# One hybrid decoder step: the scan of each SSD group cut anew

## The chip, the cores and the metric

The kernel runs on one core of a Trainium2 chip. TensorE (PE) multiplies matrices, VectorE (DVE) and ScalarE (ACT) work element by element, GpSimd (POOL) is a second, programmable element engine, and SyncE (SP) issues the DMA transfers. The metric is the device time of one execution in microseconds (us). Before the change, three runs have a median of 1921.59 us (1919.1 to 1923.15).

## What is computed

The reference is one layer of a decoder trunk on 256 prompt tokens (with 16 learned meta tokens ahead of them) and 8 x 8 sample tokens, all in float32. Cut to what matters:

```python
h = rms_norm(x, norm_w)
z, xbc, dt_raw, sc_b, sc_c, sc_h, sc_z, g_a, g_b = split_proj(h @ w_in)
xbc = silu(causal_dwconv(xbc, conv_prev, ssd_conv_w) + ssd_conv_b)
xs, bm, cm = split(xbc)                  # 64 heads x 64; 8 groups x 128 states
dt = softplus(dt_raw + dt_bias)
# per segment, chunk by chunk; acum is the running sum of dt * -exp(a_log):
y_diag = (cc . bc) * exp(seg) * dt  applied to xc        # inside the chunk
h_next = exp(acum[-1]) * h + sum(to_end * xc * bc)       # carried state
y_off  = exp(acum) * (cc . h)                            # from the state before
y = y_diag + y_off + d_skip * xs
y_a = group_rms_norm(y * silu(z)) @ w_ssd_out            # norm over 512 of one group
y_b = (sc_b * causal_dwconv(sc_c * sc_h) * silu(sc_z)) @ w_sconv_out
out = x + (sigmoid(g_a) * y_a + sigmoid(g_b) * y_b) @ w_o   # then a last rms_norm
```

The outputs also hold the new states: of the prompt, and of each of the 8 sample sequences (128 x 512 numbers a group and sequence).

## The kernel before

Activations lie transposed: 128 channels on the partitions, tokens along the columns. There are T = 336 columns: 16 meta, 256 prompt, 64 sample; TV = 320 leaves the meta tokens out. Each weight block of 128 x 1024 float32 is loaded by SyncE (`wraw`, L79), rounded by ScalarE to a high part (`whi`, L81), and VectorE makes the rest (`wlo`, L83); each has three buffers. A product is then three matmuls in fp32r, a single-pass form of float32: high by high (L89), high weight by low activation (L90), low weight by high activation (L93). One unit is 48 such matmuls.

The stage with the scan ("pb") has 8 groups of 8 heads. A group's units run in a fixed order: 4 z units (L407), 8 output units of the group before (L588; of two outputs of 24 matmuls each), and 6 conv units of the next group (L391: B, C, and four tiles of x). Group 0 has no output units; group 7 has 8 gate units (L602) in place of the conv units. The scan `ssd(g)` is a generator which yields between its steps, and `weave` (L619) runs some of its steps after each unit, `NSTEP` = 24 spread over the group's units. [...]

The scan cuts the 336 columns into three chunks of 128, 128 and 80: the first has meta and prompt, the third 16 prompt columns and the 64 sample columns. Its steps in order: `to_rows` (transposes x and B of a chunk into rows, L444, L448; `xdt` is x times dt), `weights` (the decay matrix `W`, loaded from DRAM and made by subtraction, exponent and the product with `cbm`, L462 to L465; `xe` on GpSimd, L467; `E` for the off-diagonal part of chunk 1), `inside` (the weighted sums, L477), `skip` (adds d_skip * x, L485), `carry` (the state, matmul L495, into `hst`). For the sample states `h0` (loaded at L432) the old state's contribution is taken by matmuls on `CZ` (L525; L528 does the same for the prompt columns of chunk 2), then GpSimd shrinks all eight states in place (L533), and the weighted sums of chunk 2 receive that contribution through the constant `C_SY` (L538).

The new sample states need, for each sequence, its 8 rows of x and B in four variants (high and low parts) at 32 partitions. Constant selection matrices (`sel`, matmuls L560, L561, L565, L566) do this on TensorE, for four sequences at a time. Then eight matmuls of 32 rows (L573), each with its addition to `h0` (L574), and the stores (L576), two sequences in each of four steps.

The group norm takes `zs[0]`, the sum of squares of 128 channels' lanes over four tiles. `rstd` (L105) sums over partitions by one-column matmuls (L111), so that 320 tokens lie as 112 x 3, scales them (L115, VectorE), raises them to -0.5 (L116, GpSimd), spreads them as diagonals (L121, VectorE) and multiplies by ones (L122) to have the factor in all partitions. Then y is scaled (L582) and split in high and low parts (`yh`, `yl`, L583, L584) for the output units.

PSUM has eight banks in four names of two: `pj` (projections), `ms` and `sg` (scan), `yb` (weighted sums).

Of the kernel before, what the change touches and what calls it, by code (L numbers as in the profile page):

```python
# [7 lines left out]
F32 = mybir.dt.float32  # L8
# [16 lines left out]
NSTEP = 24  # L25

C_ID, C_U, C_M1, C_UQ, C_M1Q, C_ONE = 0, 128, 256, 384, 464, 544
C_SX, C_SE, C_SY, C_SEG = 672, 1696, 1824, 1904
C_ALL = 1912
# [13 lines left out]
def tile_hybrid_step(ctx, tc, xT, w1, w2, wdt, wso, wsc, wo, cmask, vec, hvec, convst, sconvst, h0T,  # L43
# [11 lines left out]
    sg_d = dr.tile([KT, P, TV], F32, name="sg_d")  # L55

# [68 lines left out]

    def run(gen):
# [15 lines left out]
    with tc.tile_pool(name="pa", bufs=2) as pa:  # L142
# [31 lines left out]
        def eights(ap, w=8):  # L174
            return ap.rearrange("p (b t) -> p b t", t=w)

# [44 lines left out]
        consts(0, C_SX)  # L221
# [26 lines left out]
        for j in range(KT):  # L248
            u = (up0, ups0) if j == 0 else u1 if j == 1 else conv_in(j, proj)
            if j == 3:  # L250
                nc.sync.dma_start(HV, hvec)
                consts(C_SX, C_SE)
# [98 lines left out]
    def sel(kind, u):  # L351
        o = C_SX + (2 * kind + u) * P
        return CR[:80, o:o + P]

# [3 lines left out]
    with tc.tile_pool(name="pb", bufs=2) as pb:  # L358
# [4 lines left out]
        CZ = pb.tile([P, 288], F32, name="CZ", bufs=1)  # L363
        nc.gpsimd.memset(CZ, 0.0)
        czs = CZ[:, 0:256].rearrange("p (q w) -> p q w", w=64)
# [57 lines left out]
        def ssd(g, st):  # L423
# [4 lines left out]
            nc.gpsimd.tensor_copy(CZ[:, 272:288], CT[:, 256:272])  # L428
            h0, h0t = [], []
            for u in range(4):  # L430
# [4 lines left out]
            ys = [pb.tile([P, TV], F32, name="ys", bufs=4) for _ in range(4)]  # L435
            W, xdt, xe, bt, cbm, yb = [None] * 3, [None] * 3, [None] * 3, None, None, [None] * 3

            def to_rows(c):
                t0, n = CH[c]
                W[c] = pb.tile([P, 8, P], F32, name="W")  # L440
                nc.sync.dma_start(W[c][:n, :, :n], ac_d[c][8 * g:8 * g + 8, :].partition_broadcast(n))
                pp = ps.tile([P, 512], F32, name="ms")
                for t in range(4):
                    nc.tensor.transpose(pp[:n, t * P:t * P + P], xs[:, t, t0:t0 + n], ident)  # L444
                xdt[c] = big("xdt", 2)
                nc.vector.tensor_tensor(split(xdt[c][:n]), split(pp[:n]), bc(hv(dtt[:n, c, :], g), [n, 8, HP]), mult)
                pq = ps.tile([P, 512], F32, name="ms")
                nc.tensor.transpose(pq[:n, 0:P], BT[:, t0:t0 + n], ident)  # L448
                nc.tensor.matmul(pq[:n, P:P + n], BT[:, t0:t0 + n], CT[:, t0:t0 + n], start=True, stop=True)
                bt = pb.tile([P, P], F32, name="bt", bufs=1)  # L450
                nc.scalar.activation(bt[:n], pq[:n, 0:P], AF.Copy)
                cbm = pb.tile([P, P], F32, name="cbm")
                nc.vector.tensor_tensor(cbm[:n, :n], pq[:n, P:P + n], U if c < 2 else UQ, mult)
                return bt, cbm

            def weights(c):
                n, w = CH[c][1], W[c]
                if c == 1:
                    nc.scalar.activation(E, w, AF.Exp)
                    nc.gpsimd.tensor_tensor(E, E, bc(CT[:, P:2 * P].unsqueeze(1), [P, 8, P]), mult)  # L460
                for h in range(8):
                    nc.vector.tensor_scalar(w[:n, h, :n], w[:n, h, :n], act[:n, c, 8 * g + h:8 * g + h + 1], 0.0,  # L462
                                            sub, ALU.min)
                nc.scalar.activation(w[:n, :, :n], w[:n, :, :n], AF.Exp)
                nc.vector.tensor_tensor(w[:n, :, :n], w[:n, :, :n], bc(cbm[:n, :n].unsqueeze(1), [n, 8, n]), mult)  # L465
                xe[c] = big("xe", 2)
                nc.gpsimd.tensor_tensor(split(xe[c][:n]), split(xdt[c][:n]), bc(hv(tet[:n, c, :], g), [n, 8, HP]), mult)  # L467

            def inside(c):
                n = CH[c][1]  # L470
                yb[c] = ps.tile([P, 512], F32, name="yb")
                for t in range(4):
                    lhs = [(xdt[c][:n], W[c][:n, :, :n])] + ([(hst, E)] if c == 1 else [])
                    for i, (x, w) in enumerate(lhs):
                        for q in range(2):
                            h = 2 * t + q
                            nc.tensor.matmul(yb[c][q * HP:(q + 1) * HP, t * n:t * n + n],  # L477
                                             x[:, h * HP:(h + 1) * HP], w[:, h, :],
                                             start=t == 0 and i == 0, stop=t == 3 and i == len(lhs) - 1 and c < 2)

            def skip(c):
                t0, n = CH[c]
                i0 = META if c == 0 else 0
                for t in range(4):
                    nc.vector.scalar_tensor_tensor(ys[t][:, t0 + i0 - META:t0 + n - META],  # L485
                                                   xs[:, t, t0 + i0:t0 + n], col(V_D, 4 * g + t),
                                                   yb[c][:, t * n + i0:t * n + n], mult, add)

            def carry(c):
                hn = big("hst", 2)  # L490
                if c:
                    nc.gpsimd.tensor_tensor(split(hn), split(hst), bc(hv(cdec[:, c - 1, :], g), [P, 8, HP]), mult)
                r = CH[c][1] if c < 2 else META
                pst = ps.tile([P, 512], F32, name="sg")
                nc.tensor.matmul(pst, bt[:r], xe[c][:r], start=True, stop=True)  # L495
                if c == 0:
                    nc.scalar.activation(hn, pst, AF.Copy)
                else:
                    nc.vector.tensor_tensor(hn, hn, pst, add)
                return hn  # L500

            E = pb.tile([P, 8, P], F32, name="E", bufs=1)
            bt, cbm = to_rows(0)
# [3 lines left out]
            hst = carry(0)  # L507
            bt, cbm = to_rows(1)
            yield
            weights(1)  # L510
            yield
            yield
            inside(0)
            inside(1)
            skip(0)
            skip(1)
            yield
            hst = carry(1)
            bt, cbm = to_rows(2)
            yield  # L520
            weights(2)
            pp = ps.tile([P, 512], F32, name="ms")
            for s_ in range(2):
                for q in range(4):
                    nc.tensor.matmul(pp[32 * q:32 * q + 32], CZ[:, 64 * q + 32 * s_:64 * q + 32 * s_ + 32],  # L525
                                     h0[2 * q + s_], start=s_ == 0, stop=False)
            for q in range(4):
                nc.tensor.matmul(pp[32 * q:32 * q + 32, q * P:q * P + P], CZ[:, 256:288], hst[:, q * P:q * P + P],  # L528
                                 start=False, stop=True)
            yo = big("yo", 1)  # L530
            nc.vector.tensor_tensor(split(yo), split(pp), bc(hv(eaY, g), [P, 8, HP]), mult)
            for b in range(NB):
                nc.gpsimd.tensor_tensor(split(h0[b]), split(h0[b]), bc(hv(decS[:, b, :], g), [P, 8, HP]), mult)  # L533
            yield
            yield
            inside(2)
            for t in range(4):
                nc.tensor.matmul(yb[2][:, t * 80:t * 80 + 80], yo[:, t * P:t * P + P], CM[:, C_SY:C_SY + 80],  # L538
                                 start=False, stop=t == 3)
            yield  # L540
            nc.sync.dma_start(ssmp[g], carry(2))
            skip(2)
            xe = xe[2]
            xe2 = pb.tile([P, 2, 512], F32R, name="xe2", tag="W")
            xeh, xel = xe2[:, 0, :], xe2[:, 1, :]
            nc.scalar.activation(xeh[:80], xe[:80], AF.Copy)
            nc.vector.tensor_tensor(xel[:80], xe[:80], fb(xeh[:80]), sub)
            bhh = pb.tile([P, 2, P], F32R, name="bhh", bufs=1)
            nc.scalar.activation(bhh[:80, 0, :], bt[:80], AF.Copy)
            nc.vector.tensor_tensor(bhh[:80, 1, :], bt[:80], fb(bhh[:80, 0, :]), sub)  # L550
            zs = st["zs"]
            for t in range(4):
                nc.vector.tensor_tensor(ys[t], ys[t], zs[t], mult)  # L553
                nc.scalar.activation(zs[t], ys[t], AF.Square)
                if t:
                    nc.gpsimd.tensor_tensor(zs[0], zs[0], zs[t], add)
# [237 lines left out]
```

## Time and profile before

| | |
|---|---|
| median of three runs | 1921.59 us |
| profiled execution | 1921.81 us, its span 1920.0 us |
| mean granted TensorE clock | 0.994 |
| group 0, from its first matmul to that of group 1 | 96.4 us |
| groups 1 to 6, each | 119.1 to 119.2 us |
| group 7 | 118.7 us |

The span is the time from the first to the last instruction of one execution that the profiler recorded; the rest of its time lies around it. Rows of a timeline give start, duration, engine, line, operation, output <- inputs, shapes, and in brackets the idle time of the engine just before and what ended it. Matmuls overlap, so their durations are longer than the distance from one start to the next; the distance is what they cost. A group of instructions is given with its count and its shortest, median and longest duration in ns.

### The profile page before, as it was taken

To read this page: it belongs to the slowest core of one execution; us is meant where nothing else is said; L and a number is where in the kernel's file an instruction comes from. 1 tells how busy PE (TensorE), PEld (TensorE's weight loads), DVE (VectorE), ACT (ScalarE), POOL (GpSimd) and SP (SyncE) were. 2 spreads that over 40 slices of the span, in tenths; PEclk is the share of its full clock that TensorE was granted. 3 is DMA by queue.
4 is the path that set the end of the run, shared out by engine and by line. 5 is a ranking of instruction groups with operands and counts; after the bars stand their busy time and mean duration, and the time that the engine had idled before them with its cause. 6 is when DMAs were issued, how large, how long until landed. Compare 5 with 4: busy or idle time off the path is not lost.

```text
span 1920.0 us, 31901 instructions
## 1 busy us (share of the span) xinstructions
PE 1878.4 (98%) x12838; PEld 1818.0 (95%) x12838; DVE 1168.2 (61%) x1831; ACT 761.9 (40%) x1074; POOL 324.2 (17%) x397
## 2 busy tenths in 40 slices
PE   7999999999999999999999999999999998999996
PEld 7999999999999999898998989989899897999996
DVE  6745444444543337776667877677776777464543
ACT  6433333333333335354543534335353442333432
POOL 0100000000000002323213232133321332000011
PEclk9999999999999999999999999999999999999998
DMA  6444444444444455363645546455364652665553
GB/s 215 152 158 153 145 152 147 150 145 155 149 157 151 161 179 190 123 222 128 232 140 192 180 127 224 148 190 175 131 227 141 199 171 93 194 225 167 169 176 106
DMA packets 102948, 318.69 MB, mean 166 GB/s; under 512 B 16144, under 2 KB 29072, under 8 KB 102800
## 3 DMA queue, kind: packets, MB, share of 16 engines
q1 hardware_dynamic: 102800, 316.65, 50.2%
q8 instruction: 101, 1.65, 0.3%
q14 instruction: 47, 0.39, 0.1%
HBM read 290.28 MB, written 26.32 MB: 165 GB/s over the span
## 4 chain that ended last, share of the span: by engine, by line
PE 61%; DVE 5%; issue 1%; ACT 1%; DMA 1%; POOL 0%; SPq 0%; DVEq 0%; ACTq 0%
PE pj L89 19%; PE pj L90 18%; PE pj L93 18%; DVE wlo L83 1%; PE yb L477 1%; PE sg L495 1%; DVE ys L553 1%; PE ms L525 1%; DVE W L462 1%; PE sg L573 1%; DMA W<-ac_d 1%; ACT whi L81 0%; PE ms L444 0%; PE ms L122 0%; DVE ya L599 0%
## 5 line engine op out<-in xcount | busy, mean ns | idle before, releaser
L83 DVE TENSOR_TENSOR wlo<-wraw,whi 128x1024 fp32r<-128x1024 f32 x481 | 603.4, 1255 | 509.1 <-PE pj L93 315.3
L89 PE MATMUL pj<-hhi,whi 128*128 128x320 f32 (+3 forms) x2960 | 892.9, 313 | 0.0
L90 PE MATMUL pj<-hlo,whi 128*128 128x320 f32 (+3 forms) x2960 | 887.7, 312 | 0.0
L81 ACT ACTIVATE whi<-wraw 128x1024 fp32r<-128x1024 f32 x481 | 508.8, 1058 | 881.1 <-PE pj L90 809.5
L89 PEld LDWEIGHTS pj<-hhi,whi 128*128 128x128 f32 x2960 | 556.1, 188 | 4.4 <-issue 3.9
L90 PEld LDWEIGHTS pj<-hlo,whi 128*128 128x128 f32 x2960 | 555.2, 188 | 1.0 <-issue 0.7
L93 PE MATMUL pj<-hhi,wlo 128*128 128x320 f32 (+3 forms) x2960 | 501.1, 311 | 0.0
L93 PEld LDWEIGHTS pj<-hhi,wlo 128*128 128x128 f32 x2960 | 455.5, 188 | 0.5 <-issue 0.2
L89 PE MATMUL pj<-yh,whi 128*128 128x320 f32 x512 | 159.2, 322 | 10.6 <-DVE ya L599 9.5
L90 PE MATMUL pj<-yl,whi 128*128 128x320 f32 x512 | 153.1, 310 | 0.0
L89 PEld LDWEIGHTS pj<-yh,whi 128*128 128x128 f32 x512 | 96.7, 189 | 24.2 <-issue 18.3
L90 PEld LDWEIGHTS pj<-yl,whi 128*128 128x128 f32 x512 | 96.9, 189 | 0.0
L93 PE MATMUL pj<-yh,wlo 128*128 128x320 f32 x512 | 96.4, 310 | 0.0
L381 DVE SCALAR_TENSOR_TENSOR cacc<-pad,V,cacc 128x360 f32<-128x360 f32 (+1 forms) x144 | 86.4, 600 | 14.9 <-ACT cacc L379 11.5
L533 POOL TENSOR_TENSOR h<-h,decS 128x512 f32<-128x512 f32 x64 | 81.6, 1308 | 9.9 <-PE ms L525 9.9
L192 POOL COPY SCS<-up 128x2 f32<-128x2 f32 x16 | 20.5, 1281 | 368.8 <-DVE up L186 365.8
L93 PEld LDWEIGHTS pj<-yh,wlo 128*128 128x128 f32 x512 | 80.8, 189 | 0.2 <-issue 0.2
L599 DVE TENSOR_TENSOR ya<-ya,pj 128x320 f32<-128x320 f32 x112 | 54.0, 482 | 37.0 <-PE pj L93 36.8
L90 PE MATMUL pj<-vlo,whi 128*128 128x320 f32 x256 | 75.5, 309 | 0.0
L89 PE MATMUL pj<-vhi,whi 128*128 128x320 f32 x256 | 75.5, 309 | 0.0
L375 POOL COPY cs<-pad 128x3 f32<-128x3 f32 x48 | 30.6, 638 | 249.0 <-ACT pad L372 249.0
L462 DVE TENSOR_SCALAR W<-W,act 128x128 f32<-128x128 f32 (+1 forms) x192 | 55.0, 341 | 8.8 <-DMA W<-ac_d 8.0
(205 smaller groups left out, 1571.6 us busy)
## 6 DMA issues: line engine op xcount, KB each, us to landing
wraw<-w SPq DMA_DIRECT2D x352, 512.0 KB, 3.9
wraw<-wso SPq DMA_DIRECT2D x64, 512.0 KB, 3.5
wraw<-wsc SPq DMA_DIRECT2D x32, 512.0 KB, 3.7
h<-h0T SPq DMA_DIRECT2D x32, 512.0 KB, 5.4
ssms<-h SPq DMA_DIRECT2D x32, 512.0 KB, 4.7
wraw<-wo SPq DMA_DIRECT2D x32, 512.0 KB, 3.8
W<-ac_d SPq DMA_DIRECT2D x16, 512.0 KB, 6.2
mb_d<-thg SPq DMA_DIRECT2D x16, 160.0 KB, 1.8
```

The source lines that it names most:

```text
L81: nc.scalar.activation(hi[:, :n], raw[:, :n], AF.Copy)
L83: nc.vector.tensor_tensor(lo[:, :n], raw[:, :n], fb(hi[:, :n]), sub)
L89: nc.tensor.matmul(out, w, xh(k0 + k), start=first and k == 0, stop=False)
L90: nc.tensor.matmul(out, w, xl(k0 + k), start=False, stop=False)
L93: nc.tensor.matmul(out, w, xh(k0 + k), start=False, stop=last and k == nk - 1)
L192: nc.gpsimd.tensor_copy(SCS[:, j, 0, :], up[:, 256:258])
L375: nc.gpsimd.tensor_copy(cs[:, 0, :], pad[:, 272:275])
L381: nc.vector.scalar_tensor_tensor(acc[:, i0:], pad[:, i0 + k:360 + k], col(V_CW, 4 * j + k), acc[:, i0:], mult, add)
L462: nc.vector.tensor_scalar(w[:n, h, :n], w[:n, h, :n], act[:n, c, 8 * g + h:8 * g + h + 1], 0.0, sub, ALU.min)
L477: nc.tensor.matmul(yb[c][q * HP:(q + 1) * HP, t * n:t * n + n], x[:, h * HP:(h + 1) * HP], w[:, h, :], start=t == 0 and i == 0, stop=t == ...
L533: nc.gpsimd.tensor_tensor(split(h0[b]), split(h0[b]), bc(hv(decS[:, b, :], g), [P, 8, HP]), mult)
L599: nc.vector.tensor_tensor(ya[:, m, :TV], ya[:, m, :TV], pp[:, :TV], add)
```

## The change

The scan is cut into other steps, with `NSTEP` = 22:

- **One visit for all weighted sums.** The sums of the three chunks run together (L538 of the changed kernel, and L542 for the sample part) after both states are there; the banks of `yb` are one tile of two banks, and chunk 2 uses a bank of `sg`. Its part from the state before, formerly by `CZ`, now uses `E2`, an exponential matrix of 16 columns made like `E`. The d_skip additions follow (L545, L553).
- **Rows replicated through DRAM.** The high and low parts of x and B are written twice to `xq_d` and `bq_d` (L561, L562) and read back as tiles with the four variants (L574, L577). The selection matrices and their constants go. The state of the third chunk is a matmul over 64 replicated rows in fp32r (L479 by `state(2, ...)`).
- **Updates four at a time.** Four matmuls (L588) into four banks, `ms` and `sg` in turn, then four additions (L590) and two stores (L593), in one step for each half.
- **The norm by a matmul of ones.** 128 x 128 ones times `zs[0]` (L596) gives the sum in all partitions; VectorE scales 128 x 320 (L598), GpSimd raises 128 x 320 to -0.5 (L599), and VectorE scales y with the result (L606).
- The shrinks (L487) are issued in four pairs in four steps. Gate units 0 to 3 move to group 0, which then has 14 units, and group 7 has 16.

```diff
-NSTEP = 24
+NSTEP = 22
+    xq_d = [dr.tile([80, 4, 512], F32, name=f"xq_d{i}") for i in range(2)]
+    bq_d = [dr.tile([80, 4, P], F32, name=f"bq_d{i}") for i in range(2)]
...
+            def state(c, lhs, rhs, tag):
+                pst = ps.tile([P, 512], F32, name=tag)
+                nc.tensor.matmul(pst, lhs, rhs, start=True, stop=True)
+                if c:
+                    nc.vector.tensor_tensor(hst[c], hst[c], pst, add)
+                else:
+                    nc.scalar.activation(hst[c], pst, AF.Copy)
...
-            for q in range(4):
-                nc.tensor.matmul(pp[32 * q:32 * q + 32, q * P:q * P + P], CZ[:, 256:288], hst[:, q * P:q * P + P],
-                                 start=False, stop=True)
...
+            yb = ps.tile([P, 2, 512], F32, name="yb", bufs=1)
+            yq = ps.tile([P, 512], F32, name="sg")
+            for c, (t0, n) in enumerate(CH):
+                y = yb[:, c, :] if c < 2 else yq
+                off = [None, (hst[0], E, P), (hst[1], E2, META)][c]
                 for t in range(4):
+                    lhs = [(xdt[c][:n], W[c][:n, :, :n], n)] + ([off] if c else [])
+                    for i, (x, w, m) in enumerate(lhs):
                         for q in range(2):
                             h = 2 * t + q
+                            nc.tensor.matmul(y[q * HP:(q + 1) * HP, t * n:t * n + m],
+                                             x[:, h * HP:(h + 1) * HP], w[:, h, :], start=t == 0 and i == 0,
+                                             stop=t == 3 and i == len(lhs) - 1 and c < 2)
...
+            xq, bq = xq_d[g % 2], bq_d[g % 2]
+            for r in range(2):
+                nc.sync.dma_start(xq[:, 2 * r:2 * r + 2, :], fb(xe2[:80]))
+                nc.sync.dma_start(bq[:, r:r + 3:2, :], fb(bhh[:80]))
...
-            for u in range(2):
-                pp = ps.tile([P, 512], F32, name="ms")
-                nc.tensor.matmul(pp, sel(0, u), xeh[:80], start=True, stop=False)
-                nc.tensor.matmul(pp, sel(1, u), xel[:80], start=False, stop=True)
-                xh = big("xdt", 2, F32R)
-                nc.scalar.activation(xh, pp, AF.Copy)
...
+            for d, q in ((x3, xq), (b3, bq)):
+                nc.sync.dma_start(fb(d[:64]), q[:16].rearrange("p r c -> (p r) c"))
+            for d, q in ((xh, xq), (bh, bq)):
+                for u in range(2):
+                    nc.sync.dma_start(fb(d[:, u, :]), q[16 + 32 * u:48 + 32 * u].rearrange("p r c -> (p r) c"))
...
+            state(2, b3[:64], x3[:64], "sg")
+            nc.sync.dma_start(ssmp[g], hst[2])
+            for u in range(2):
+                up = [ps.tile([P, 512], F32, name="sg" if b % 2 else "ms") for b in range(4)]
+                for b in range(4):
+                    q = slice(32 * b, 32 * b + 32)
+                    nc.tensor.matmul(up[b], bh[q, u, :], xh[q, u, :], start=True, stop=True)
+                for b in range(4):
+                    nc.vector.tensor_tensor(h0[4 * u + b], h0[4 * u + b], up[b], add)
                 yield
...
-            rs = yield from rstd(pb, [zs[0]], META, 1.0 / 512, 4.0 * EPS)
+            pt_ = ps.tile([P, 512], F32, name="ms")
+            nc.tensor.matmul(pt_[:, :TV], ones, zs[0], start=True, stop=True)
+            rs = pb.tile([P, TV], F32, name="rs_m", bufs=1)
+            nc.vector.tensor_scalar(rs, pt_[:, :TV], 1.0 / 512, 4.0 * EPS, mult, add)
+            nc.gpsimd.tensor_tensor(rs, rs, bc(mhalf, [P, TV]), ALU.pow)
+            yield
+            yield
...
+            if g in (0, NG - 1):
+                parts.append(gate_units(0, 4) if g == 0 else gate_units(4, 8))
+                n += 4
```

Three places show how the order moves. The first is VectorE at the norm of a steady group, among the conv tiles (`pad`, `cacc`, `cth`) of the next group's x and the weight splits `wlo`. Before:

```order
L115 TENSOR_SCALAR rs_m<-ms 112x3 [waits PE_49]
L381 SCALAR_TENSOR_TENSOR cacc<-pad_6687,V,cacc 128x360 [waits Activation_49]
L121 TENSOR_SCALAR rs_d<-CR,rs_r 112x112 [waits Pool_49]
L381 SCALAR_TENSOR_TENSOR cacc<-pad_6687,V,cacc 128x360 [waits DVE_49]
L121 TENSOR_SCALAR rs_d<-CR,rs_r 112x112
L381 SCALAR_TENSOR_TENSOR cacc<-pad_6687,V,cacc 128x360 [waits DVE_49]
L83 TENSOR_TENSOR wlo<-wraw,whi 128x1024 [waits DMAHW7_49,PE_49,Activation_49]
L385 SCALAR_TENSOR_TENSOR xs<-cth,cacc 128x272 [waits Activation_49]
L386 SCALAR_TENSOR_TENSOR xs<-cth,cacc 128x64
L83 TENSOR_TENSOR wlo<-wraw,whi 128x1024 [waits DMAHW1_49,PE_49,Activation_49]
```

VectorE waits here for GpSimd's power of 112 x 3 (`rs_r`) after one accumulate of the conv. In the changed kernel:

```order
L85 TENSOR_TENSOR wlo<-wraw,whi 128x1024 [waits DMAHW0_49,PE_49,Activation_49]
L598 TENSOR_SCALAR rs_m<-ms 128x320 [waits PE_49]
L378 SCALAR_TENSOR_TENSOR cacc<-pad_6688,V,cacc 128x360 [waits Activation_49]
L606 SCALAR_TENSOR_TENSOR ys<-ys,V,rs_m 128x320 [waits Pool_49]
L378 SCALAR_TENSOR_TENSOR cacc<-pad_6688,V,cacc 128x360 [waits DVE_49]
L606 SCALAR_TENSOR_TENSOR ys<-ys,V,rs_m 128x320
L378 SCALAR_TENSOR_TENSOR cacc<-pad_6688,V,cacc 128x360 [waits DVE_49]
L608 TENSOR_TENSOR yl<-ys,yh 128x320 [waits Activation_49]
```

The scaling of y (L606) has moved up to the place behind one accumulate, and waits there for the power of 128 x 320.

The second place is SyncE's queue in a steady group around the reads of the replicated rows. Before, weight loads (L79) stand among the decay loads (L441) and the stores of the states (L541, L576):

```order
L441 DMA W<-ac_d_66 128x1024 [waits PE_49]
L79 DMA wraw<-w 128x1024 [waits DMAHW0_49,DVE_49]
L79 DMA wraw<-w 128x1024 [waits DMAHW1_49,DVE_49]
L541 DMA ssmp<-hst 128x512 [waits DVE_49,Pool_49]
L79 DMA wraw<-w 128x1024 [waits DMAHW7_49,DMAHW2_49,DVE_49]
L576 DMA ssms<-h_9491 128x1024 [waits DVE_49]
```

In the changed kernel, with `xq_d` the copy of x in DRAM, `xdt` (for x3) and `xh` the tiles read from it:

```order
L433 DMA W_9717<-ac_d_68 128x640 [waits PE_49]
L561 DMA xq_d_72<-xe_9030 80x1024 [waits DMAHW0_49,DVE_49]
L561 DMA xq_d_72<-xe_9030 80x1024 [waits DMAHW1_49]
L81 DMA wraw<-w 128x1024 [waits DMAHW4_49,DMAHW2_49,DVE_49]
L574 DMA xdt<-xq_d_72 64x512 [waits DMAHW1_49,DMAHW0_49,Pool_49]
L577 DMA xh<-xq_d_72 128x512
L577 DMA xh<-xq_d_72 128x512 [waits DMAHW5_49]
L81 DMA wraw<-w 128x1024 [waits DMAHW6_49,DVE_49]
```

The reads stand between two weight loads and wait for the writes.

The third place is TensorE in the changed kernel where the first updates run, between projections of a C tile (128x324) and an x tile (128x336):

```order
L95 MATMUL pj<-hhi,wlo 128x324 x7
L479 MATMUL sg<-xdt,b_9125 128x512 [waits DMAHW3_49,DMAHW0_49]
L588 MATMUL ms<-xh,bh 128x512 [waits DMAHW4_49,DMAHW1_49]
L588 MATMUL sg<-xh,bh 128x512 [waits PE_49]
L588 MATMUL ms<-xh,bh 128x512
L91 MATMUL pj<-hhi,whi 128x336 [waits PE_49,Activation_49]
L92 MATMUL pj<-hlo,whi 128x336
L588 MATMUL sg<-xh,bh 128x512 [waits DVE_49]
```

The third chunk's state and three updates share a visit, and the fourth update comes two projection matmuls later, once VectorE has read its bank.

More of the change, by code (lines that the diff above doesn't have):

```diff
@@ L481, in skip @@
[L481 to L500, printed above, removed]
@@ L534, in ssd @@
+            for t in range(1, 4):
+                nc.gpsimd.tensor_tensor(zs[0], zs[0], zs[t], add)
             yield
             yield
[L536 to L539, printed above, removed]
-            yield
[L541 to L544, printed above, removed]
```

242 lines of the change are left out of this document (127 added, 115 removed).

## The prediction

> **What bounds the kernel now.** I read the page's engine shares first, then the chain of work that ended last, then the windows of three scan groups.
>
> ```profile
> PE 1878.4 (98%) x12838; PEld 1818.0 (95%) x12838; DVE 1168.2 (61%) x1831; ACT 761.9 (40%) x1074; POOL 324.2 (17%) x397
> PE 61%; DVE 5%; issue 1%; ACT 1%; DMA 1%; POOL 0%; SPq 0%; DVEq 0%; ACTq 0%
> 760.00:856.40 96.40, 92.11 (x632) 83.75 (x631) 76.35 (x128) 42.38 (x71) 32.89 (x40) 1.00 0.52 171
> 1094.70:1213.80 119.10, 118.64 (x825) 111.89 (x824) 87.52 (x152) 51.71 (x79) 34.32 (x40) 1.00 0.54 174
> 1571.10:1689.80 118.70, 111.12 (x776) 104.13 (x775) 73.65 (x104) 38.76 (x55) 18.43 (x17) 0.97 0.46 147
> ```
>
> TensorE is busy for 98% of the span and leads every other engine in the chain. The windows are group 0, group 3 (the groups from 1 to 6 are alike) and group 7; their columns are length, then busy time of PE, PEld, DVE, ACT and POOL, then clock, DMA share and GB/s. In group 3 TensorE is busy for 118.64 of 119.10 us, so whatever matmul time the scan gives up there shortens the group, as long as no wait takes its place. In group 7 it is busy for 111.12 of 118.70 us: there a wait is to be had.
>
> The bulk of a group is projections. Their matmuls start one pitch apart:
>
> ```profile
> 1183.11 0.66 PE L111 MATMUL ms<-CR,zs 128*112 128x1 f32 x6
> ...
> 1183.87 0.32 PE L90 MATMUL pj<-hlo,whi 128*128 128x336 f32 x1
> ...
> 1185.10 0.32 PE L90 MATMUL pj<-hlo,whi 128*128 128x336 f32 x1
> ...
> 1191.13 0.59 PE L122 MATMUL ms<-rs_d,CR 112*128 112x112 f32 x4
> ...
> 1191.73 0.32 PE L90 MATMUL pj<-hlo,whi 128*128 128x336 f32 x1
> ...
> 1192.65 0.32 PE L90 MATMUL pj<-hlo,whi 128*128 128x336 f32 x1
> 1192.86 0.47 PE L122 MATMUL ms<-rs_d,CR 112*128 112x112 f32 x2
> ...
> 1193.34 0.32 PE L90 MATMUL pj<-hlo,whi 128*128 128x336 f32 x1
> ```
>
> Eight pitches from 1183.87 to 1185.10 make 0.154 us for 336 columns; by the columns that is 0.147 for 320 and 0.149 for 324. A steady group has 384 matmuls of 320, 240 of 336 and 48 of 324, together 100.6 us, so the scan and its waits cost 119.1 - 100.6 = **18.5 us**. Group 0 has 480 (72.4 us), which leaves 24.0; group 7 has 624 of 320 columns (91.7 us), which leaves 27.0. The change touches these 18.5, 24.0 and 27.0 us; the rest of the kernel I leave as it is.
>
> **The change part by part.** A scan visit costs the distance between the projection matmuls around it, less one pitch.
>
> The norm first, in the rows above. Its three visits cost 1183.87 - 0.154 - 1183.11 = 0.61, then 1191.73 - 0.154 - 1191.13 = 0.45, and 1193.34 - 0.154 - (1192.65 + 0.154) = 0.38 behind the matmul of 1192.65: 1.44 in all. The new norm is one float32 matmul of 320 columns.
>
> ```profile
> 1102.55 1.02 PE L495 MATMUL sg<-xe,bt 128*128 128x512 f32 x2
> 1103.40 0.60 PE L444 MATMUL ms<-CR,xs 128*128 128x128 f32 x4
> ...
> 1131.72 0.40 PE L528 MATMUL ms<-hst,CZ 128*32 128x128 f32 x8
> ...
> 1135.77 0.78 PE L477 MATMUL yb<-W,xdt 80*64 80x80 f32 x16
> ...
> 1140.42 0.75 PE L93 MATMUL pj<-yh,wlo 128*128 128x320 f32 x4
> 1141.10 1.12 PE L495 MATMUL sg<-xe,bt 16*128 16x512 f32 x2
> ...
> 1142.40 0.31 PE L90 MATMUL pj<-yl,whi 128*128 128x320 f32 x1
> ```
>
> A float32 matmul of 512 columns runs as two passes and takes 1103.40 - 1102.55 = 0.85, so 320 columns take 0.53: norm **-0.9**. The third chunk's state, 16 rows in float32, occupies 1140.42 + 4 x 0.147 = 1141.01 to 1142.40 - 0.147 = 1142.25, that is 1.24. The eight short matmuls on the meta chunk's columns (L528), busy for 0.40 with their pipelined end, go; without that end I count **-0.2**. What takes their place are sixteen matmuls of 16 columns (on E2) in the large visit. Sixteen of 80 columns start at 1135.77 and are through at 1136.47, 0.70; sixteen of 16 columns cost between a fifth of that and all of it, 0.14 to 0.70, and I take **+0.5**, near the upper end, since such short ones hardly cover their own weight loads.
>
> ```profile
> 1159.19 0.40 PE L560 MATMUL ms<-xe,CR 80*128 80x512 f32 x1
> 1159.43 0.39 PE L561 MATMUL ms<-xe,CR 80*128 80x512 f32 x1
> ...
> 1160.03 0.32 PE L90 MATMUL pj<-hlo,whi 128*128 128x336 f32 x1
> ...
> 912.10 0.75 PE L93 MATMUL pj<-yh,wlo 128*128 128x320 f32 x4
> 912.78 0.50 PE L573 MATMUL sg<-xdt,bh 32*128 32x512 f32 x2
> ...
> 913.46 0.31 PE L90 MATMUL pj<-yl,whi 128*128 128x320 f32 x1
> ```
>
> A selection visit (L560 to L566) costs 1160.03 - 0.154 - 1159.19 = 0.69; both go, **-1.4**, since DMA now replicates the rows. The new state reads replicated rows in one fp32r pass: 0.24 by the distance of L560 and L561, and 0.1 for the changeover, against 1.24: **-0.9**. An update visit costs 913.46 - 0.147 - (912.10 + 4 x 0.147) = 0.62, and there are four; afterwards I count three, because the first updates share the state's visit, and 0.2 for the one whose bank is still being read by the state's addition: **-0.4**. Steps that share a visit save about 0.1 each, **-0.2**. The sum is -0.9 - 0.2 + 0.5 - 1.4 - 0.9 - 0.4 - 0.2 = **-3.5 us** for a steady group, which leaves 15.0 of the 18.5.
>
> Group 0 now has 14 units instead of 10 beside its scan, since four gate units come forward. I put its scan at 15.6, the steady rest and 0.6 of waits: **-8.4**. Group 7 has a wait of its own:
>
> ```profile
> 1608.96 9.66 DVE L465 TENSOR_TENSOR W<-W,cbm 80x640 f32<-80x640 f32 x1
> 1609.90 8.04 POOL L533 TENSOR_TENSOR h<-h,decS 128x512 f32<-128x512 f32 x8
> 1620.37 0.61 PE L89 MATMUL pj<-yh,whi 128*128 128x320 f32 x1 [7.58 <-DVE ya L599]
> ssmp<-hst SPq DMA_DIRECT2D x8, 256.0 KB, 4.2
> h<-h0T SPq DMA_DIRECT2D x32, 512.0 KB, 5.4
> SPq L79 <- DVE wlo L83: 1174.0, 391, 14.2
> ```
>
> The eight shrinks of GpSimd run back to back for 8.04 us, VectorE's product stands still beside them for 9.66, and TensorE waits for 7.58. The new order issues the shrinks in pairs, so this goes. What may come instead is the trip through DRAM: about 4.5 us of VectorE work ahead of it, a write of about 4.2 (the row of ssmp), and reads of 0.7 to issue and 5.4 to land (the row of h0T), 14.8 in all. In a steady group the updates come 144 projection matmuls after the large visit, 21.6 us, which hides it; in group 7 they come 72 later, 10.6 us, so TensorE waits for about 4: 27.0 becomes 15.6 + 4 = 19.6, **-7.4**. SyncE keeps the weight loads queued behind the new transfers, but its own queue spends 1174 us waiting for VectorE's splits, so those loads run ahead. The dropped constants in the first stage cost nothing either way: they were loaded beside TensorE work.
>
> Without the power this is 6 x -3.5 - 8.4 - 7.4 = -36.8 us.
>
> **The power.** GpSimd now raises 128 x 320 elements to -0.5, where it did 112 x 3. Nothing in the trace shows that size.
>
> ```profile
> L116 POOL TENSOR_TENSOR rs_r<-rs_m,mhalf x10: 850/858/879, 38.1 to 1904.9; 112x3 f32<-112x3 f32 x10
> L556 POOL TENSOR_TENSOR zs<-zs x24: 862/1004/1497, 798.9 to 1633.5; 128x320 f32<-128x320 f32 x24
> L533 POOL TENSOR_TENSOR h<-h,decS x64: 1035/1042/2027, 784.7 to 1616.9; 128x512 f32<-128x512 f32 x64
> 1193.37 0.55 DVE L582 SCALAR_TENSOR_TENSOR ys<-ys,V,ms 128x320 f32<-128x320 f32 x1
> ...
> 1199.61 1.23 DVE L83 TENSOR_TENSOR wlo<-wraw,whi 128x1024 fp32r<-128x1024 f32 x1
> ...
> 1208.37 1.85 DVE L381 SCALAR_TENSOR_TENSOR cacc<-pad,V,cacc 128x360 f32<-128x360 f32 x3
> ...
> 1212.05 0.22 DVE L386 SCALAR_TENSOR_TENSOR xs<-cth,cacc 128x64 f32<-128x64 f32 x1
> ```
>
> Call its time D. From below it is the power of three columns, 0.86 us. From above: the plain operations of 320 and 512 columns take 0.862 and 1.035 at least, so 0.0009 a column on a fixed 0.57; the 0.858 of the power then holds 0.28 for three columns, and if each column costs its 0.095 anew, D is 0.57 + 30.4 = 31 us. I take **D = 4**: between those ends the nearest row is the one of equal shape and engine, 1.0, and the power must be dearer than an addition; the middle of the ends by ratio would be 5.2.
>
> [...]
>
> What D does: VectorE's scaling of y (L606) waits for it, and it stands right behind rs_m in VectorE's order, with the conv of the next group's x and two weight splits behind it. With the norm visit at zero, VectorE does a split and rs_m until 2.0; the power runs until 2.0 + D; then come rows like those from 1193.37 to 1199.61 and the split that ends them, 6.2 + 1.2 = 7.4; then the accumulate and the output of the last conv tile, 1208.37 to 1212.27, 3.9. So x is there at 13.3 + D. TensorE asks for it after the visit's 0.54, 48 matmuls of 0.154 and 48 of 0.147, and 0.33 of earlier transposes: 15.3. The wait is **D - 2.0** where that is positive, 2.0 us by my D, in every group (in group 7 the output units wait for y in the same way): 8 x 2.0 = +16.0. Each further microsecond of D costs 8.
>
> Sum: -36.8 + 16.0 = -20.8. The profiled execution took 1921.81 us (span 1920.0 and 1.8 around it), 0.2 above the median of the three runs, so the forecast is **1901 us**.
>
> **The rivals.**
> *The power is long, and its wait outgrows everything that was saved.* The mechanism is the one above, at one place: L606 in VectorE's queue. It decides from a wait of 36.8 / 8 = 4.6, so from D = 6.6 us. With D = 15, the middle by ratio between 7 and 31, the wait is 13 and the time 1885 + 104 = 1989; with D = 31 it is 2117. For it speaks that three columns already take as long as 320 of an addition; against it, that the time of three columns may be nearly all fixed.
> *GpSimd's work locks VectorE out in each group as it did once in group 7.* The shrinks are in pairs now, but the state's carry, xe and E2 stand near them. The price there is a wait of 7.58 and about 2 us of half clock behind it, 9.6; in seven groups +67, so 1968. Against it: group 3, with the same eight shrinks in a row, leaves TensorE idle for 119.10 - 118.64 = 0.46 us only. [...]
> *The trip through DRAM is late in every group*, by another 4 us as in group 7: +28, 1929 with D = 4, and the change would have given its gain away. Against it stand 21.6 us of cover for 14.8.
> *D under 2*: no wait at all, 1885.
>
> **How the numbers follow.** The power at up to 6.6 us, with the trip hidden, has 0.55: D is spread evenly by ratio from 0.86 to 31, and 6.6 lies a little past the middle. The long power has 0.35, the lock-out and the late trip 0.05 each. About 0.2% is what a measurement of this kernel can tell from no change, here 3.8 us: D between 6.1 and 7.1 stays within it. So faster 0.52, the same 0.06, slower 0.42. The likeliest case alone reaches from 1873 (no wait, cheap E2, updates side by side, -1.5 in each group) to 1922. The range goes down to **1870** and up to **2000** (D = 16.4); beyond it lies a power of more than 16 us, about 0.18.
>
> **What the profile afterwards would show.** The row of the power at L599 gives D at once. If I am right, TensorE's wait at the next group's transposes (L439, ended by VectorE's xs) is near 2 us, the group windows are 117.6 long, group 0's is longer by its four units (96.4 - 8.4 + 192 x 0.147 + 2.0 = 118.2), and the wait for DVE ya at L623 in group 7 is gone. A wait of PE on the reads of xh in groups 0 to 6 would say that the trip isn't hidden; DVE rows of several microseconds beside GpSimd's would say lock-out. I am wrong if D is above 6.6, or if the wait does not follow D - 2.0.

## The result, and the profile after

The changed kernel takes **2296.4 us** (median of four runs, 2292.58 to 2299.1); before, beside it, 1922.37 us. The ratio is 1.194, 95% interval 1.192 to 1.196. The forecast was 1901 us with a range to 2000.

The first three rows are the page of the changed kernel: engine shares, the TensorE clock in 40 slices, and the chain that ended last by engine. Below them are two steady groups of its windows, each from one norm to the next (columns as in the prediction).

```profile
PE 1871.0 (82%) x12750; PEld 1823.2 (79%) x12750; DVE 1150.2 (50%) x1774; ACT 749.5 (33%) x1050; POOL 715.9 (31%) x397
PEclk9999999999999996995995995996996986978998
PE 16%; POOL 5%; DVE 1%; DMA 1%; issue 0%; ACT 0%; SPq 0%; DVEq 0%; ACTq 0%
```

```profile
1025.26:1192.89 167.63, 118.69 (x814) 113.48 (x813) 86.98 (x145) 48.11 (x74) 81.91 (x40) 0.85 0.39 132
1192.89:1362.46 169.57, 117.77 (x814) 112.42 (x813) 88.41 (x146) 51.96 (x77) 83.86 (x41) 0.85 0.39 135
```

TensorE has fallen from 98% to 82% of the span without having more to do, and GpSimd's busy time has risen by 392 us, about as much as the kernel became longer. The two steady groups last 167.6 and 169.6 us instead of 119.1, and in the first of them TensorE is idle for 48.9 us. The group of the power's instructions (shortest, median, longest in ns) and the list of waits (total, times, longest) name the place:

```profile
L599 POOL TENSOR_TENSOR rs_m<-rs_m,mhalf x8: 51327/51328/51621, 859.5 to 2021.2; 128x320 f32<-128x320 f32 x8
```

```profile
ACT yh L607 <- DVE ys L606: 417.9, 21, 53.3
DVE ys L606 <- POOL rs_m L599: 404.1, 8, 51.4
...
PE pj L91 <- ACT whi L83: 330.3, 7, 48.9
PE pj L91 <- ACT yh L607: 46.7, 1, 46.7
PE ms L439 <- DVE xs L382: 18.0, 7, 4.8
```

The power of 128 x 320 takes **51.3 us**, eight times. VectorE stands still for 404 us at the scaling of y, ScalarE behind it at the rounding of y, and with ScalarE its next task, the rounding of the weights that TensorE needs. In group 7, which has no conv units, TensorE waits for the rounded y itself (`yh`). The timelines of GpSimd, VectorE, ScalarE and TensorE in one group show the four links:

```profile
1030.30 51.33 POOL L599 TENSOR_TENSOR rs_m<-rs_m,mhalf 128x320 f32<-128x320 f32 x1
```

```profile
1030.82 0.59 DVE L378 SCALAR_TENSOR_TENSOR cacc<-pad,V,cacc 128x360 f32<-128x360 f32 x1 [0.84 <-ACT cacc L376]
1081.66 0.55 DVE L606 SCALAR_TENSOR_TENSOR ys<-ys,V,rs_m 128x320 f32<-128x320 f32 x1 [50.24 <-POOL rs_m L599]
```

```profile
1082.24 0.47 ACT L607 ACTIVATE yh<-ys 128x320 fp32r<-128x320 f32 x1 [51.45 <-DVE ys L606]
1082.62 1.04 ACT L83 ACTIVATE whi<-wraw 128x1024 fp32r<-128x1024 f32 x1
```

```profile
1083.71 0.63 PE L91 MATMUL pj<-hhi,whi 128*128 128x320 f32 x1 [46.82 <-ACT whi L83]
1084.14 0.47 PE L92 MATMUL pj<-hlo,whi 128*128 128x320 f32 x1
1084.41 0.47 PE L91 MATMUL pj<-hhi,whi 128*128 128x320 f32 x1
...
1092.28 0.47 PE L439 MATMUL ms<-CR,xs 128*128 128x128 f32 x1 [2.13 <-DVE xs L382]
```

TensorE waits 46.8 us for the weights and 2.1 at the transposes, 48.95 together. After the long wait its matmuls start 0.27 us apart (1084.14 to 1084.41) where 0.147 is the usual pitch. The granted clock is 0.50 from 1083.71 to 1088.14 and 1.00 from 1089.00 to the end of the second wait; behind that wait the longer pitch comes back until 1095.60, at a clock of 0.51. From 1083.71 to there the mean is 0.64, and the page shows such dips through all of the scan groups.

### The profile page after: what moved, and what is told of

It is laid out like the page before. It is cut to its first block, busy times and chain, and to the rows that moved or that the text cites. A ratio compares the mean times of both kernels' runs of the same rounds, so it can differ in the third digit from the quotient of the medians.

```text
span 2294.4 us, 31773 instructions
## 1 busy us (share of the span) xinstructions
PE 1871.0 (82%) x12750; PEld 1823.2 (79%) x12750; DVE 1150.2 (50%) x1774; ACT 749.5 (33%) x1050; POOL 715.9 (31%) x397
## 5 line engine op out<-in xcount | busy, mean ns | idle before, releaser
L91 PE MATMUL pj<-hhi,whi 128*128 128x320 f32 (+3 forms) x2960 | 907.4, 318 | 330.3 <-ACT whi L83 330.3
L92 PE MATMUL pj<-hlo,whi 128*128 128x320 f32 (+3 forms) x2960 | 900.6, 316 | 0.0
L91 PEld LDWEIGHTS pj<-hhi,whi 128*128 128x128 f32 x2960 | 567.1, 192 | 339.8 <-ACT whi L83 332.2
L92 PEld LDWEIGHTS pj<-hlo,whi 128*128 128x128 f32 x2960 | 566.8, 191 | 1.8 <-issue 0.9
L599 POOL TENSOR_TENSOR rs_m<-rs_m,mhalf 128x320 f32<-128x320 f32 x8 | 410.9, 51365 | 32.6 <-DVE rs_m L598 32.6
L606 DVE SCALAR_TENSOR_TENSOR ys<-ys,V,rs_m 128x320 f32<-128x320 f32 x32 | 17.4, 548 | 404.1 <-POOL rs_m L599 404.1
L91 PE MATMUL pj<-yh,whi 128*128 128x320 f32 x512 | 158.5, 321 | 46.7 <-ACT yh L607 46.7
L607 ACT ACTIVATE yh<-ys 128x320 fp32r<-128x320 f32 x32 | 14.7, 465 | 417.9 <-DVE ys L606 417.9
L487 POOL TENSOR_TENSOR h<-h,decS 128x512 f32<-128x512 f32 x64 | 72.3, 1166 | 57.3 <-PE ms L517 57.3
```

Of the source, the lines that this page charges most:

```text
L91: nc.tensor.matmul(out, w, xh(k0 + k), start=first and k == 0, stop=False)
L92: nc.tensor.matmul(out, w, xl(k0 + k), start=False, stop=False)
L599: nc.gpsimd.tensor_tensor(rs, rs, bc(mhalf, [P, TV]), ALU.pow)
L606: nc.vector.scalar_tensor_tensor(y, y, col(V_SNW, 4 * g + t), rs, mult, mult)
```

## The experiments

Ratios are to the kernel before in runs beside each other, with the 95% interval.

**1. A multiplication in place of the power.**

```diff
-            nc.gpsimd.tensor_tensor(rs, rs, bc(mhalf, [P, TV]), ALU.pow)
+            nc.gpsimd.tensor_tensor(rs, rs, bc(mhalf, [P, TV]), mult)
```

> The changed kernel with a multiplication in place of the power, on the same engine, operands and shape; the power is left out, so y is scaled by another factor. Theory A (the whole loss is the wait for the power, D - 2.0 us in each of eight groups): the operation takes about 1.0 us like the addition of that shape, no wait is left, 1885 us as in the sum on record without the power, within 10. Rival B (the recut itself also loses: the trip through DRAM, the joined visits, GpSimd beside VectorE): 1915 us or more, with other waits of TensorE of over 1 us a group.

Measured: 1888.92 us, ratio 0.981 (0.979 to 0.982). The operation's row, the window of five steady groups from norm to norm, and VectorE and TensorE after the second of these norms:

```profile
L599 POOL TENSOR_TENSOR rs_m<-rs_m,mhalf x8: 721/722/999, 864.5 to 1667.6; 128x320 f32<-128x320 f32 x8
```

```profile
979.51:1558.93 579.42, 572.75 (x4063) 548.06 (x4062) 435.31 (x725) 248.25 (x375) 160.07 (x199) 1.00 0.59 193
```

```profile
1094.59 3.88 DVE L457 TENSOR_SCALAR W<-W,act 128x128 f32<-128x128 f32 x8 [1.86 <-ACT E L453]
1098.39 1.21 DVE L85 TENSOR_TENSOR wlo<-wraw,whi 128x1024 fp32r<-128x1024 f32 x1
1099.53 0.48 DVE L598 TENSOR_SCALAR rs_m<-ms 128x320 f32<-128x320 f32 x1
```

```profile
1094.47 0.70 PE L596 MATMUL ms<-zs,CR 128*128 128x320 f32 x2
...
1111.97 0.33 PE L439 MATMUL ms<-CR,xs 128*128 128x128 f32 x1 [2.01 <-DVE xs L382]
```

Without the power the recut is worth 35.5 us (1924.45 - 1888.92), and the whole loss is the power: theory A, against rival B. The two profiles, 2294.4 and 1888.7 us long, account for it on TensorE: its waits behind the power are 384 us longer in the changed kernel (330.3 + 46.7 + 18.0 + 1.1, the last for `yl`, against 11.7), and the same 12750 matmuls are busy for 22 us more, at the longer pitch.

One thing disagrees with theory A. With D = 0.72 there should be no wait at the transposes, and there is one of 2.0 us in the group shown, 11.7 us in seven groups. The rows say why: between the norm's matmul at 1094.47 and rs_m at 1099.53 VectorE first does eight decay subtractions (3.88 us), so that rs_m is done 5.5 us after the norm and not 2.0. In this group VectorE does not wait for GpSimd (in all eight it does for 1.4 us):

```profile
1100.32 0.72 POOL L599 TENSOR_TENSOR rs_m<-rs_m,mhalf 128x320 f32<-128x320 f32 x1
```

```profile
1100.85 0.59 DVE L378 SCALAR_TENSOR_TENSOR cacc<-pad,V,cacc 128x360 f32<-128x360 f32 x1 [0.84 <-ACT cacc L376]
1101.36 0.55 DVE L606 SCALAR_TENSOR_TENSOR ys<-ys,V,rs_m 128x320 f32<-128x320 f32 x1
```

At this D the wait comes from what stands ahead of the conv in VectorE's queue.

**2. The old norm in the changed kernel.**

```diff
-            pt_ = ps.tile([P, 512], F32, name="ms")
-            nc.tensor.matmul(pt_[:, :TV], ones, zs[0], start=True, stop=True)
...
-            nc.gpsimd.tensor_tensor(rs, rs, bc(mhalf, [P, TV]), ALU.pow)
-            yield
-            yield
+            rs = yield from rstd(pb, [zs[0]], META, 1.0 / 512, 4.0 * EPS)
```

> The changed kernel with the norm of before (sums by one-column matmuls, power of 112x3, diagonals). Theory A: the run with the multiplication plus what three short visits cost over one, 8 x 0.9 = 7 us, so about 1892 us, faster than before by 1.5%. Rival B: 1920 us or more.

Measured: 1901.87 us, ratio 0.988 (0.986 to 0.990). Faster than before, as A has it, though 10 us behind its figure. TensorE's timeline shows a wait that A had not counted:

```profile
987.44 0.47 PE L124 MATMUL ms<-rs_d,CR 112*128 112x112 f32 x2 [1.13 <-DVE rs_d L123]
```

The third diagonal is late, and TensorE waits for diagonals for 15.9 us in all. The kernel gives the diagonals two buffers, so the third takes that of the first; with a third buffer (experiment 10) 2.2 us are left of the 15.9.

**3. The power on 32 of 320 columns.**

```diff
+            nc.gpsimd.tensor_tensor(rs[:, :32], rs[:, :32], bc(mhalf, [P, 32]), ALU.pow)
+            nc.gpsimd.tensor_tensor(rs[:, 32:], rs[:, 32:], bc(mhalf, [P, TV - 32]), mult)
```

> The changed kernel with the power on 32 of the 320 columns and a multiplication on the other 288 (the power of those is left out). If the power costs 0.38 us and 0.159 us a column (from 0.858 us for 3 and 51.33 us for 320), the two operations take 5.5 + 1.0 = 6.5 us. Theory A, a wait of D - 2.0: 4.5 us a group, 36 us over the run with the multiplication. Rival C (the engines run far enough ahead that a wait of a few us is swallowed, and only a long one hurts): under 10 us over it.

Measured: 1940.32 us, ratio 1.008 (1.006 to 1.010), 51 us over the multiplication where theory A had 36. Its two operations:

```profile
L599 POOL TENSOR_TENSOR rs_m<-rs_m,mhalf x8: 5424/5426/5716, 860.0 to 1705.8; 128x32 f32<-128x32 f32 x8
```

```profile
L600 POOL TENSOR_TENSOR rs_m<-rs_m,mhalf x8: 663/667/668, 865.7 to 1711.2; 128x288 f32<-128x288 f32 x8
```

The price of the power is a straight line: 0.858 us for 3 columns, 5.43 for 32, 51.33 for 320, 0.159 a column on a fixed 0.4 ((51.33 - 5.43) / 288 and 0.858 - 3 x 0.159). Rival C falls: D is 5.43 + 0.67 = 6.1, 5.4 more than in experiment 1, and the time 51.4 us more, 6.4 in each of eight groups. That is more than D grew by, and waiting is only a part of it. Between the two profiled executions, 44 us apart, TensorE's waits behind the power grow by 31 us, from 11.7 to 42.9, and its matmuls are busy for 13.6 us more. In a straight line between the two runs the 35.5 us are used up at D of about 0.7 + 35.5 / 8 / (6.4 / 5.4) = 4.4 us, an estimate, where the prediction had 6.6.

**4. Only the new norm, in the kernel before.** The edit puts the matmul of ones and the power of 128x320 where the kernel before calls `rstd`.

> The kernel before with only its norm replaced by the matmul of ones and the power of 128x320. Theory A: all of the loss comes from this step, whatever the rest of the scan looks like: 8 x 49.3 us of wait, 8 x 2 us of half clock behind it, less 8 x 0.9 us of shorter visits, so about 1922 + 403 = 2325 us. Rival D (the wait is long only where the changed kernel issues the norm, one unit of 7 us later): 8 x 7 less, about 2270 us.

Measured: 2297.12 us, ratio 1.193 (1.190 to 1.195). With none of the rest of the recut, the loss is as large as that of the whole change (1.194). It lies halfway between the two figures, at 46.6 us a group. TensorE's waits behind the power are 45.1 us a group here (361.0 in all) against 49.5 in the changed kernel; that the earlier place saves these 4 us is likely but not shown.

**5. The old norm with sums and power issued earlier.** Two steps lie between the power and the diagonals.

```diff
+            norm = rstd(pb, [zs[0]], META, 1.0 / 512, 4.0 * EPS)
             for u in range(2):
+                if u:
+                    next(norm)
...
-            rs = yield from rstd(pb, [zs[0]], META, 1.0 / 512, 4.0 * EPS)
+            rs = yield from norm
```

> The changed kernel with the norm of before, whose sums and power of 112x3 are issued ahead of the second four updates, two steps before its diagonals. Theory A: what the run with the old norm lost against the one with the multiplication (12.9 us) is mostly TensorE's wait for the diagonals (15.9 us in all), so this ends within 5 us of the multiplication, at about 1890 us, and computes everything. Rival E (the loss is the two extra visits and VectorE's diagonals themselves): it stays at 1898 us or more.

Measured: 1899.42 us, ratio 0.987 (0.986 to 0.989), the same as experiment 2 within the intervals. TensorE's wait for the diagonals is still there in the list of waits:

```profile
PE ms L124 <- DVE rs_d L123: 13.9, 8, 2.6
```

The power's place was not the cause; the third diagonal's buffer is independent of it.

**6. The scaling of y issued four units later.** `finish` holds the scaling and splitting, chained behind the next group's z units; the tiles `ys` are also allocated later, just ahead of the weighted sums.

```diff
+                parts.append(finish(g - 1, S[g - 1]))
                 parts.append(out_units(g - 1, S[g - 1]))
```

> The changed kernel, with its power of 128x320, but the scaling and splitting of y issued behind the next group's four z units. Theory A as the prediction had it (what hurts is the place of the scaling in VectorE's queue): four units of 7.1 us more cover, seven or eight times 28 us less, about 2080 us. Rival F (GpSimd's own queue is as bad: the copies for the next conv tile stand behind the power and VectorE's accumulates behind those): only the scaling's few us leave the chain, 3 to 6 us a group, 2250 to 2275 us.

Measured: 2296.53 us, ratio 1.194 (1.192 to 1.197): no change at all, which neither theory had. The order of VectorE's instructions in this kernel, where the scaling has become L611, tells why:

```
L598 TENSOR_SCALAR rs_m<-ms 128x320 [waits PE_49]
L378 SCALAR_TENSOR_TENSOR cacc<-pad_6688,V,cacc 128x360 [waits Activation_49]
L611 SCALAR_TENSOR_TENSOR ys<-ys,V,rs_m 128x320 [waits Pool_49]
L378 SCALAR_TENSOR_TENSOR cacc<-pad_6688,V,cacc 128x360 [waits DVE_49]
L611 SCALAR_TENSOR_TENSOR ys<-ys,V,rs_m 128x320
```

The scaling stands where it stood. An engine's order in the built program is thus not simply the order in which the code issues the work, and the yields alone do not set what stands behind what. The run does not tell the two theories apart.

**7 (run e9). The scaling tied to the fourth z tile,** by a factor that reads it.

```diff
+                nc.vector.scalar_tensor_tensor(w4, S[g + 1]["zs"][3][:, 0:4], 0.0, w, mult, add)
...
-                nc.vector.scalar_tensor_tensor(y, y, col(V_SNW, 4 * g + t), rs, mult, mult)
+                nc.vector.scalar_tensor_tensor(y, y, w[:, t:t + 1], rs, mult, mult)
```

> The changed kernel with its power of 128x320, and the scaling of y tied to the next group's fourth z tile by a factor that reads it, so that it truly stands behind four units of projections (group 7 has none and stays as it is). Theory A as the prediction had it (what hurts is the place of the scaling in VectorE's and ScalarE's queues): 28 us more cover in seven groups, 2296 - 7 x 28 = 2100 us. Rival F (GpSimd's queue is as bad: the pad copy of the next conv tile, with VectorE's accumulates waiting for it, stands behind the power): the wait stays above 40 us a group, 2240 to 2290 us.

Measured: 2262.51 us, ratio 1.176 (1.173 to 1.178). The added dependence moves the scaling behind the four units, which issuing it later did not, and still only 34 us are gained: rival F's figure, though not by the path that it named. The last conv tile is finished during the power here. VectorE, GpSimd, SyncE and TensorE in one group:

```profile
1035.57 0.43 DVE L382 SCALAR_TENSOR_TENSOR xs<-cth,cacc 128x272 f32<-128x272 f32 x1
```

```profile
1027.13 51.33 POOL L599 TENSOR_TENSOR rs_m<-rs_m,mhalf 128x320 f32<-128x320 f32 x1
...
1078.68 0.20 POOL L373 COPY cs<-pad 128x24 f32<-128x24 f32 x1
```

```profile
1026.45 4.55 SPq L81 DMA_DIRECT2D wraw<-w  x2
1078.91 0.34 SPq L402 DMA_DIRECT2D convo<-cs  x1
1079.35 0.38 SPq L81 DMA_DIRECT2D wraw<-w  x1
```

```profile
1085.51 0.64 PE L91 MATMUL pj<-hhi,whi 128*128 128x320 f32 x1 [35.52 <-ACT whi L83]
```

The store of the conv state (`convo`, L402) waits for a small copy of GpSimd that stands behind the power, and the weight loads stand behind that store in SyncE's queue: no load is issued from 1031 to 1079. ScalarE's rounding, which TensorE waits for, in its turn waits for those loads, as the list of waits has it:

```profile
ACT whi L83 <- DMA wraw<-w: 344.9, 22, 47.7
```

The long power blocks the kernel through two queues; taking VectorE's wait away uncovers SyncE's.

**8 (run e7). All eight gate units in group 7,** with the old norm. The gate's first four units also use another staging tile.

> The changed kernel with the norm of before, and all eight gate units in group 7 as before. By the sum on record group 0 gained 8.4 us, 5 of these by its four extra units; group 7 loses its wait of 1.7 us for the rows from DRAM when it has four more units. So 2 to 5 us over the run with the old norm, about 1905 us. Rival: within 1.5 us of it, since projections moved from one group to another cost the same and group 0's waits had another cause.

Measured: 1907.35 us, ratio 0.992 (0.990 to 0.994), against 0.988 with the units moved: 5.5 us longer by the medians and 8 by the ratios, above the 2 to 5 expected. That the total comes near is in part luck. From its first z tile to that of group 1, group 0 takes 94.0 us here and 118.1 in experiment 2; its four gate units are 28.2 of that (192 x 0.147), so moving them there saves 4.1 where the sum had 5. Groups 1 to 6, which the edit was not meant to touch, last 8.3 us longer together, with 5.2 us more of TensorE's wait for the diagonals, and what follows them is 3.2 us shorter, apart from the four units; TensorE no longer waits there for the rows from DRAM (1.4 us in experiment 2).

**9 (run e8). Only the rows through DRAM, in the kernel before.** The selection matmuls and their copies go, the writes and reads of `xq_d` and `bq_d` come in.

> The kernel before, with only the selection matmuls replaced by rows replicated through DRAM (the third chunk's state stays as it was). By the sum on record two visits of 0.69 us go in each of eight groups, 11 us, so about 1911 us, if the trip is hidden: it takes about 11 us from the first write to the landing of the last read in the changed kernel, and here three steps of 5.3 us cover it. Rival: the updates wait for the reads, several us a group, and the time is 1922 us or more.

Measured: 1914.34 us, ratio 0.996 (0.994 to 0.997). This part alone gains 0.4%, 8 to 10 us of the 11 expected, and TensorE waits for none of the reads.

**10 to 12 (runs e10, e11, e12). A third buffer for the diagonals:** with the old norm in the changed kernel, the same with the sums issued earlier, and in the kernel before.

```diff
-            dg = pool.tile([P, P], F32, name="rs_d", tag="cbm", bufs=2)
+            dg = pool.tile([P, T // 3], F32, name="rs_d", bufs=3)
```

> The changed kernel with the norm of before and a third buffer for the diagonals. Theory G (what TensorE waits for in the run with the old norm is the third diagonal, whose buffer is free only after the first product): 1.2 us a group less than that run, about 1892 us. Rival: VectorE is late with all three, and the wait moves to the first diagonal: 1898 us or more.

> As the run before it, with sums and power of 112x3 issued ahead of the second four updates. Theory G: no wait for diagonals is left, so the run with the multiplication plus the cost of two visits more, 0.9 us a group: 1889 + 4 to 7, about 1894 us. Rival: the same 1899 us as with two buffers, if the split of the updates around the sums is what costs.

> The kernel before with a third buffer for the norm's diagonals and nothing else. If the recut is what the last two runs gained from, this gives only the joining of two product visits, 0.4 us in each of eight groups and 3 us in all, about 1920 us. Rival: the third buffer alone explains a good part of the 40 us, 1900 us or less.

Measured: 1884.42 us, ratio 0.979 (0.978 to 0.980); 1883.90 us, 0.979 (0.978 to 0.981); and 1921.71 us, 0.999 (0.998 to 1.000). In the first of them the three products run in one visit, with no wait ahead of it:

```profile
982.60 0.82 PE L124 MATMUL ms<-rs_d,CR 112*128 112x112 f32 x6
983.19 0.39 PE L91 MATMUL pj<-hhi,whi 128*128 128x320 f32 x1
```

The recut with the old norm and one more buffer beats both kernels, by 2.1% and by 18%. The buffer alone gives the kernel before 0.1%: there too the third product comes in a visit of its own, behind other matmuls (1192.86 in the prediction's rows), but TensorE has no wait ahead of it. Issuing the sums earlier adds nothing.

Theory G is right about the wait and wrong about the size: both runs are 8 to 10 us below its figures, and even below the multiplication, which has no diagonals. The multiplication's wait at the transposes and that of the first of these runs show a second gain:

```profile
PE ms L439 <- DVE xs L382: 11.7, 7, 2.7
```

```profile
PE ms L439 <- DVE xs L382: 0.5, 1, 0.5
```

So the transposes hardly wait any more. VectorE's order is another one there: it finishes a whole conv tile between the diagonals and the first scaling of y, where the multiplication's rows have a scaling behind one accumulate. That this order is the reason was not tested by itself.

## Why the prediction was wrong

**The step that failed is the size of D.** "I take D = 4" was 51.3, and the upper end of 31 us was no bound. It rested on a fixed part of 0.57 us read off an addition and a multiplication and taken away from the power's 0.858 us, which left 0.095 a column. The fixed part is 0.4 and a column costs 0.159 (experiment 3). An extrapolation that takes nothing away, 0.858 / 3 x 320 = 91.5 us, would have been a bound, and the measured value lies between the two. The choice within the range then leaned on the row of equal shape and engine; but that row is an addition, and the row of equal operation, three columns as long as 320 of an addition, was the nearer one.

**The rival named the mechanism.** The long power with its wait at L606 is what happened, and the formula 1885 + 8 x (51.3 - 2.0) gives 2279 against 2296. It leaves out the longer pitch after each wait, about 22 us of matmul time. The rival had a chance of 0.35, and within it a D above 16 was left outside the range. Of the links, the one that TensorE waits for is ScalarE's weight rounding behind y's (46.8 us), and the transposes of x, which the prediction named, are the rest (2.1 us). So the path was wrong in part: the working followed VectorE's conv to x and left out ScalarE, whose queue holds the weight rounding behind the rounding of y.

**The slack of 2.0 was wrong for a short power.** The norm's rs_m stands behind eight decay subtractions of 3.88 us, which the working left out. TensorE's waits behind the power are 1.5 us a group at D = 0.72, 5.4 at 6.1 and 49.5 at 51.3; D - 2.0 gives none, 4.1 and 49.3. With the slower matmuls on top, the gain is used up at about 4.4 us of D, not at 6.6. Had D been 4, the change would have been worth almost nothing.

**The rest of the sum held.** Without the power 1885 us was forecast against 1888.92 measured, and 119.1 - 3.5 = 115.6 us for a steady group against 579.42 / 5 = 115.9 in the window of experiment 1. Since that holds a wait of 1.7 us on average (11.7 us in seven groups) which the sum did not count, the visits themselves must have become cheaper than forecast by about as much, and that the totals agree so closely is partly luck; the single terms were not taken apart by runs, but for the rows through DRAM. For E2 the sum had +0.5, since such short matmuls hardly cover their weight loads: in one group of the changed kernel sixteen of 80 columns and sixteen of 16 take 1.08 us together (1144.66 to 1145.74), 0.38 more than the 0.70 of before, and four of the short ones cost 0.09 us (1144.80 to 1144.89) where their four loads take 0.13 (1144.73 to 1144.86). TensorE's only wait for the trip through DRAM in the changed kernel is in group 7, 1.5 us where 4 were forecast, and experiment 9 has none. The four gate units save 4.1 us in group 0 (experiment 8). GpSimd's pairs of shrinks locked nothing out that the traces show: VectorE's longest product with `cbm` (L463) takes 1.97 us in the changed kernel, where one took 9.66 before. That rival, and the late trip, did not happen.

## What to carry to other kernels

An operation that a profile shows only at a small size has no price until its cost per element is known: extrapolate it without taking off a fixed part for the upper end, and if that end decides the sign, the change is not to be forecast from the nearer-looking row of another operation. A factor that is needed in all partitions was cheaper here raised once for each token, 112 x 3 in 0.86 us, and spread by matmuls (1884 us), than raised in 128 partitions at once (2296 us). When a long instruction sits in one engine's queue, list the consumers in every queue, the DMA issuer's too, before moving one of them.

## What the runs showed of the hardware that was not expected

GpSimd's power costs 0.159 us for each column of 112 or 128 partitions, over 3, 32 and 320 columns, while its multiplication of the same 320 takes 0.72 us in all: a factor of 71. And after a wait of 46.8 us TensorE starts its 320-column matmuls 0.267 us apart instead of 0.147 for 4.4 us, at a granted clock of 0.50, and again for 3.3 us behind the second wait of 2.1 us, at 0.51; after the 7.58 us in the kernel before this lasts 3.2 us (1620.37 to 1623.52), at 0.54.
